# Four head pairs' chains in lockstep instead of two, one chunk a step, and the two directions' outputs stored apart

## The chip, the cores and the metric

The kernel runs on one core of a Trainium2 chip. Its time is the device time of the whole program in microseconds (us): the median of three runs, with the lowest and highest beside it. One further execution was recorded by the hardware profiler. Engines carry the profile's names: PE is the matrix engine (PEld its weight loads), DVE, ACT and POOL the vector, scalar and general engines, SP the queue that issues most loads.

## What is computed

One layer of a backbone over 1024 latent tokens with a prefix of 256 context tokens, width 1024, all in float32. Two branches read the same normalised input; the change touches the first, a bidirectional RWKV-7 scan with 16 heads of 64:

```
def step(S, inp):                                   # one token, state S of 64 x 64 per head
    sa = einsum('bhvk,bhk->bhv', S, kk_t)
    S  = S * w_t - sa b_t + v_t k_t
    o  = einsum('bhvk,bhk->bhv', S, r_t)            # latents only
...
for d in (0, 1):                                    # forward, backward
    S, o = rwkv7_scan(..., S0[d], reverse=(d == 1))
o = head_norm(outs[0] + outs[1], ln_w, ln_b, 16 heads, eps)
o = o + bons[0] + bons[1]
ya = (o * silu(g)) @ w_o
```

The latent scans start from the final state of the context scan of the same direction. The second branch is a retention with four heads, in both directions, with its own norm, gate and projection. Both are merged by two gates, projected, added to the input and normalised.

## The kernel before

**Stages, in order.** Projections of the input and the preparation of the RWKV operands (to about 830 us of the span); the RWKV chains over the context (830 to 1164) together with the projection of retention's values (`gv`); the RWKV chains over the latents (1164 to 1794) together with the gate projections (`gm`); the output stage with retention and the RWKV output projection (1794 to about 2211); the merge and the last projection (to 2497).

**Chains.** The scan runs in chunks of 64 tokens: four chunks of context and sixteen of latents for each head pair and direction. The 16 heads are 8 pairs of two heads, which share the 128 partitions; a pair and a direction make one chain, so there are 16 chains. `chain_step` takes several chains one chunk further. It multiplies the old state by the keys (`X`), ACT negates the result (`xs`), `U` multiplies by the inverse of the chunk's triangular matrix (`T`), ACT copies that (`uv`), `S` and `O` make the new state and the outputs from it, and DVE adds the decayed old state `sp`, which POOL made. These depend on each other one after the other.

**Filling the waits.** Between X, U and S/O stands a gap each: `gap` puts a share of the gate projections' matmuls there, so that PE has work while ACT and DVE copy. The share is the work left over the gaps left. `rwkv_lat` takes two pairs in both directions at a time, four chains, two chunks to a group: 4 x 8 groups of two steps, 64 steps in all. With each step it puts work for the next group: `chunk_mats` (the products `A` of keys with keys and queries, from tiles `ka` and `bk`, evacuated by DVE into `ka` and `aa`, and the scaling of `bk` on POOL), `chunk_turn` (four transposes `bt` of that `bk`, evacuated by ACT), and in `inv_gap` pieces of the inverses that are needed some steps later. `inv_gap` counts gaps, 24 to an inverse: keys (`B`, from `kt` and `bi` tiles) at five of them, the vector work spread over 24 (17 in the first), and two joins (`I`). `inverse` does the same in the context stage; it waits two turns between the vector work and the join.

**Outputs.** `put` copies a finished group's outputs from PSUM into a tile `oT` of two pairs and all 1024 tokens. Whichever direction comes second in a place is added there by DVE. After eight groups `oT` is stored to `oD`, which so holds the sum of both directions.

**The output stage.** `out_a` takes the 1024 tokens in two batches of 512. In each, `rwkv_norm` runs for the eight head pairs: load the tile `ar` from `oD`, split it into two parts (`hi` on ACT, `lo` on POOL), sum over the heads on PE (`mu`, two matmuls), subtract, square, split again, sum (`va`), and scale; then two loads named `bg` (the bonus `bonD` and the gate `gD`), which POOL adds and multiplies. Eight results (`act`) feed the matmuls `ya`. Retention (`st`, `sc`, `ro`, `ktp`, `ot` on PE) stands in the same stage, and the order of the two on each engine is made by a scheduler from the order of recording, priorities and what waits for what; inside the chains the order is that of the code. `bg` tiles have the tag `"ma"` with two buffers, `ar` has two, `hi` and `lo` three.

Of the kernel before, what the change touches and what calls it, by code (L numbers as in the profile page):

```python
# [15 lines left out]
P = 128  # L16
# [33 lines left out]
MF = 2.0  # L50
# [3 lines left out]
VEC = 2.8  # L54
# [74 lines left out]
class Kern:  # L129
# [11 lines left out]
    def run(self, upto=9):  # L141
        nc, tc, ins = self.nc, self.tc, self.ins
        with ExitStack() as ctx:
# [27 lines left out]
            self.oD = dr("oD", [NPAIR, P, LAT])  # L171
# [407 lines left out]
    def phase1b(self):  # L579
        nc, tc = self.nc, self.tc  # L580
        pool = lambda name, **k: tc.tile_pool(name=name, bufs=1, reuse_waits="tile", **k)
        with ExitStack() as c:
# [22 lines left out]
            with pool("wg") as self.wp:  # L605
                self.begin(gates, 3 * 16 * NPAIR // 2, 0.0)
                self.rwkv_lat(*first)
                self.end()

    def begin(self, jobs, gaps, hold):  # L610

        self.left = sum(10 * KT * 3 * 0.107 if size == 2 else 2 * KT * 3 * 0.2135 for size, _ in jobs)
        self.debt, self.gaps, self.hold = 0.0, gaps, hold
        self.work, self.stores = self.filler(jobs), []
        next(self.work)

    def end(self):
        for _ in self.work:
            pass
        self.flush()  # L620
# [73 lines left out]
    def gate_out(self, acc, dst, silu, sp, eng=None):  # L694
# [8 lines left out]
        else:  # L703
            self.stores.append((dst, st))

    def flush(self):

        for dst, st in self.stores:
            self.nc.scalar.dma_start(dst, st)
        self.stores = []  # L710
# [86 lines left out]
    def subs(self, n):  # L797
# [3 lines left out]
        pp, half = divmod(n - 2, 2)  # L801
        return [(p, d, NCU + 8 * half + 4 * q) for q in range(2) for p in (2 * pp, 2 * pp + 1) for d in range(2)]

    def inverse(self, n):
# [146 lines left out]
    def inv_gap(self, t):  # L951
# [4 lines left out]
        per, g = divmod(t, 24)  # L956
        last = 1 + NPAIR
        n = 4 + per
        if g == 1 and n <= last:
# [8 lines left out]
        if t == 0 or g == 17:  # L968
            n = 3 + per + (g == 17)
            self.vec = self.inv_vec(self.jobs[n]) if n <= last else iter(())  # L970
            self.vec_us, self.vec_gaps, self.owed = 12 * TV + sum(map(self.sub_us, range(31))), 24 if t else 17, 0.0
# [6 lines left out]
        if g == 16:  # L978
# [3 lines left out]
    def chunk_loads(self, p, u0, d=None, extra=False):  # L982
# [4 lines left out]
        odd = p % 2 if d is None else d  # L987
        ka = (self.wp if extra else rw).tile([P, 3, 4, C], F32, tag=f"ka{odd}", name=self.nm("ka"), bufs=2 - extra)
# [6 lines left out]
        two = lambda t: t.rearrange("q (d u) c -> q d u c", d=2)  # L995
        nc.sync.dma_start(two(bk), self.bkD[p].rearrange("d q u c -> q d u c")[:, :, u0:u0 + 2, :])
        o = C * (u0 - NCU)
        kr = lambda rows, a: self.krD[p, :, rows, a, o:o + 2 * C].rearrange("d q j -> q d j")
        pair = lambda t: t.rearrange("q (d u) c -> q d (u c)", d=2)
        for h, ch, va in self.HEADS:  # L1000
            nc.sync.dma_start(pair(ka[ch, 2 * h]), kr(ch, 0))
        nc.sync.dma_start(pair(ka[:, 1]), kr(slice(0, P), 1))
        scale = self.pc[:, p, :, u0:u0 + 2].rearrange("q d (u o) -> q d u o", o=1)
        return bk, ka, scale, False

    def chunk_mats(self, loads):
# [5 lines left out]
        if ctx:  # L1012
# [6 lines left out]
            nc.gpsimd.tensor_tensor(bk, bk, scale.broadcast_to([P, 4, 2 * C]), op=ALU.mult)  # L1019
        else:  # L1020
# [11 lines left out]
            b4 = bk.rearrange("q (d u) c -> q d u c", d=2)  # L1032
            nc.gpsimd.tensor_tensor(b4, b4, scale.broadcast_to([P, 2, 2, 2 * C]), op=ALU.mult)
# [13 lines left out]
    def chain_step(self, chains, sv, uv, pcs, extra, new=None, out=None):  # L1047
# [4 lines left out]
        nc, rw = self.nc, self.rw  # L1052
        px = self.pC.tile([P, 4, C], F32, tag="C", name=self.nm("X"))
# [3 lines left out]
        xs = rw.tile([P, 4, C], F32, tag="xs", name=self.nm("xs"), bufs=1)  # L1057
        with self.tc.high_priority(offset=URGENT):
            self.lead("a", nc.scalar.mul(xs, px, -1.0))
        if new is not None:  # L1060
            sp = rw.tile([P, 4, C], F32, tag="sp", name=self.nm("sp"), bufs=1)
# [534 lines left out]
```

## Time and profile before

| | |
|---|---|
| median of 3 runs | 2504.42 us (2503.66 to 2504.76) |
| the profiled execution | 2498.37 us |
| its span | 2496.6 us |
| mean granted PE clock | 0.987 |
| busy PE, PEld | 2386.0, 1926.1 us |
| busy DVE, ACT, POOL | 1649.2, 1162.1, 562.3 us |

The profile is one execution. Busy times of an engine are shares of the span; a PE instruction's duration includes time in which it overlaps the next one, so two starts tell more than a duration. In rows of instruction groups stand the line of the kernel, the engine, the operation with output and inputs, the shapes, the count, the busy time, the mean in ns, and the idle time just before with what ended it. Line 556 is the helper that records all matmuls of the chains and gates, so those are told apart by their tiles. Lines after the edited ones shift by a few in the changed kernel (1316 becomes 1311).

### The profile page before, as it was taken

Reading aid. Unit: us, or ns where it says so; the run is one execution under the profiler, and the core shown is the slowest. Engines: PE = TensorE matmul, PEld = TensorE weight load, DVE = VectorE, ACT = ScalarE, POOL = GpSimd, SP = SyncE. Lnnn points to the kernel's source line nnn. Section 1 sums busy time; section 2 is a strip of 40 time slices with the busy share of each in tenths; the row PEclk is TensorE's granted clock in tenths of the full one; section 3 lists DMA queues with packets and bytes.
Section 4 is the critical chain, followed back from the end, with each engine's and each line's share of the span. In section 5 each row is a group of like instructions: output and inputs, shape, how many; then the busy total and the mean of one; then the engine's idle time right before and its main releaser. Section 6 shows DMA issues by size and latency. Waiting matters only on the chain.

```text
span 2496.6 us, 53437 instructions
## 1 busy us (share of the span) xinstructions
PE 2386.0 (96%) x21200; PEld 1926.1 (77%) x21200; DVE 1649.2 (66%) x2882; ACT 1162.1 (47%) x2547; POOL 562.3 (23%) x688
## 2 busy tenths in 40 slices
PE   7999999999999899997999999999898998999998
PEld 4888888777888899986777777777666765678786
DVE  5497897797796254434887787884378657754644
ACT  6434334334334334444655666554356435543422
POOL 2211021211021001211222322222276335400000
PEclk9999999999999899998999999999999999999999
DMA  6143344343344625354546556554465755585552
GB/s 250 50 149 118 140 152 135 133 141 121 135 156 152 199 88 146 106 139 124 157 145 175 163 170 192 149 160 135 123 187 165 224 160 156 180 285 170 182 174 85
DMA packets 335660, 385.07 MB, mean 154 GB/s; under 512 B 86954, under 2 KB 240306, under 8 KB 331314
## 3 DMA queue, kind: packets, MB, share of 16 engines
q1 hardware_dynamic: 304370, 298.80, 39.0%
q0 software_dynamic: 10944, 55.58, 6.7%
q10 hardware_dynamic: 20096, 27.27, 3.1%
q8 instruction: 167, 2.74, 0.4%
q14 instruction: 83, 0.68, 0.1%
HBM read 264.63 MB, written 116.92 MB: 153 GB/s over the span
## 4 chain that ended last, share of the span: by engine, by line
PE 53%; DMA 5%; DVE 5%; ACT 3%; issue 2%; SPq 2%; POOL 2%; ACTq 0%; DVEq 0%; POOLq 0%
PE gm L556 10%; PE gv L556 7%; PE ro L1475 3%; PE A L556 2%; PE yr L1276 2%; PE yr L1274 2%; PE yr L1275 2%; DMA bi<-bkD 2%; PE S L556 2%; PE X L556 2%; PE bt L1043 2%; PE gm L330 2%; PE gm L332 1%; PE gm L331 1%; PE U L556 1%
## 5 line engine op out<-in xcount | busy, mean ns | idle before, releaser
L330 PE MATMUL gm<-uh,wh 128*128 128x512 f32 x896 | 354.2, 396 | 16.2 <-ACT xp L402 13.7
L331 PE MATMUL gm<-ul,wh 128*128 128x512 f32 x896 | 353.7, 395 | 0.7 <-DVE ul L299 0.7
L332 PE MATMUL gm<-uh,wl 128*128 128x512 f32 x896 | 353.2, 394 | 0.0
L330 PEld LDWEIGHTS gm<-uh,wh 128*128 128x128 f32 x896 | 169.6, 190 | 51.5 <-ACT xp L402 15.0
L1063 POOL TENSOR_TENSOR sp<-sv,pc 64x256 f32<-64x256 f32 x152 | 104.9, 690 | 424.9 <-DVE sv L1087 202.3
L331 PEld LDWEIGHTS gm<-ul,wh 128*128 128x128 f32 x896 | 169.8, 189 | 38.4 <-DVE xnt L298 1.7
L332 PEld LDWEIGHTS gm<-uh,wl 128*128 128x128 f32 x896 | 169.7, 189 | 34.9
L556 PE MATMUL gm<-uh,wlo 128*128 128x512 f32 x416 | 171.0, 411 | 0.7 <-DVE wlo L658 0.7
L556 PE MATMUL gm<-ul,whi 128*128 128x512 f32 x416 | 171.3, 412 | 0.0
L556 PE MATMUL gm<-uh,whi 128*128 128x512 f32 x416 | 170.8, 411 | 0.0
L658 DVE TENSOR_TENSOR wlo<-wraw,whi 128x256 fp32r<-128x256 f32 x168 | 81.0, 496 | 122.5 <-ACT whi L657 121.3
L556 PE MATMUL gv<-whi,uh 128*128 128x256 f32 x512 | 148.7, 290 | 0.3 <-issue 0.3
L211 DVE TENSOR_TENSOR lo<-raw,hi 128x512 fp32r<-128x512 f32 x128 | 92.3, 726 | 85.2 <-ACT hi L210 85.0
L556 PE MATMUL gv<-whi,ul 128*128 128x256 f32 x512 | 147.7, 289 | 0.0
L556 PE MATMUL gv<-wlo,uh 128*128 128x256 f32 x512 | 147.6, 288 | 0.0
L210 ACT CAST hi<-raw 128x512 fp32r<-128x512 f32 x128 | 78.6, 620 | 140.1 <-PE yr L1275 74.1
L902 DVE TENSOR_TENSOR TL<-TL,tmp 128x31 f32<-128x31 f32 (+15 forms) x310 | 135.3, 436 | 8.5
L1077 ACT COPY uv<-U 64x256 f32<-64x256 f32 x160 | 58.6, 366 | 156.3 <-PE U L556 82.7
L900 DVE TENSOR_TENSOR tmp<-E,TL 128x31 f32<-128x31 f32 (+15 forms) x310 | 124.0, 400 | 8.9
L1087 DVE TENSOR_TENSOR sv<-S,sp 64x256 f32<-64x256 f32 x144 | 60.7, 422 | 103.1 <-PE S L556 58.6
L1475 PE MATMUL ro<-s,rs 128*128 128x512 f32 x256 | 123.7, 596 | 4.8 <-DVE s L1429 4.3
L210 ACT CAST wh<-wr 128x1024 fp32r<-128x1024 f32 x56 | 58.8, 1050 | 130.7 <-PE gm L331 127.2
(298 smaller groups left out, 6228.1 us busy)
## 6 DMA issues: line engine op xcount, KB each, us to landing
wr<-in_w_in SPq DMA_DIRECT2D x56, 512.0 KB, 3.5
wraw<-in_w_in SPq DMA_DIRECT2D x84, 256.0 KB, 3.6
bkD<-bk POOLq DMA_DIRECT2D x16, 1280.0 KB, 5.6
bk<-bkD SPq DMA_DIRECT2D x80, 256.0 KB, 3.6
krD<-kr POOLq DMA_DIRECT2D x16, 1024.0 KB, 4.4
raw<-in_wr SPq DMA_DIRECT2D x64, 256.0 KB, 3.1
vtD<-vt POOLq DMA_DIRECT2D x64, 160.0 KB, 3.9
bi<-bkD SPq DMA_DIRECT2D x160, 64.0 KB, 2.6
```

What stands on the lines that cost most here:

```text
L210: nc.scalar.copy(hi, src)
L211: (eng or nc.vector).tensor_tensor(lo, src, hi.bitcast(F32), op=ALU.subtract)
L330: nc.tensor.matmul(acc[:, :n], hi[:, k, :], self.hi(k, t0, n), start=(k == 0), stop=False)
L331: nc.tensor.matmul(acc[:, :n], hi[:, k, :], self.lo(k, t0, n), start=False, stop=False)
L332: nc.tensor.matmul(acc[:, :n], lo[:, k, :], self.hi(k, t0, n), start=False, stop=(k == KT - 1))
L556: return self.pin(self.nc.tensor.matmul(*a, **k))
L658: self.late(nc.vector.tensor_tensor(lo[:, j % size, k:k + 2], r, h.bitcast(F32), op=ALU.subtract), "v")
L900: self.late(nc.vector.tensor_tensor(t3, et[:, j + 1:, j:j + 1].broadcast_to([P, n, m]), tl[:, j:j + 1, 0:m].broadcast_to([P, n, m]), op=AL ...
L902: self.late(nc.vector.tensor_tensor(tl[:, j + 1:, 0:m], tl[:, j + 1:, 0:m], t3, op=ALU.subtract), "v")
L1063: nc.gpsimd.tensor_tensor(sp[ch], sv[ch, h], pcs[ch].broadcast_to([64, 4, C]), op=ALU.mult)
L1087: self.lead("v", nc.vector.tensor_tensor(new[h], ps[ch], sp[ch], op=ALU.add))
L1475: nc.tensor.matmul(po, qx[d][:, k, cols], st[:, k, :], start=(d == 1 and k == 0), stop=False)
```

## The change

**Latents.** `rwkv_lat` takes four pairs in both directions, eight chains, one chunk to a step: 32 steps in place of 64. The order within a step is X, then the first half of the next step's `chunk_mats` and both transposes of the tiles made a step ago, a gap; U and O, the second half of `chunk_mats` and the loads for two steps ahead, a gap; S and O, the outputs, a gap. There are 96 gaps in place of 192, and `inv_gap` counts 12 to an inverse. The transposes of a tile stand a step later than its products now. One `ka`/`bk` tile holds two pairs in both directions at one chunk, not one pair at two chunks, so the loads' contiguous pieces in DRAM halve. The tiles `sv`, `uv`, `xs`, `sp` and the PSUM tiles hold eight chains.

**A.** Each product of 128 x 128 is issued as two with 64 output partitions each, which lie in different parts of the tile of `pA`.

**Outputs.** `oD` has a plane for each direction. `put` copies both directions with ACT into a tile `og` of two steps (the backward one with its tokens reversed); `send` stores it on POOL's queue a step later, with four stores to a tile, 64 in all. `rwkv_norm` loads both planes, the second into a tile `back`, and POOL adds them; `back` has the tag `"ma"`.

**Constants and timing.** `MF` (gate work in the prologue of the latents) 2.0 to 5.0, `VEC` 2.8 to 4.2, the first fill of the first inverse in the contexts 2.5 times as long, five idle turns instead of two before an inverse's join, and stores of gate results two gaps later.

```diff
-MF = 2.0
+MF = 5.0
-VEC = 2.8
+VEC = 4.2
-            self.oD = dr("oD", [NPAIR, P, LAT])
+            self.oD = dr("oD", [2, NPAIR, P, LAT])
-                self.begin(gates, 3 * 16 * NPAIR // 2, 0.0)
+                self.begin(gates, 3 * 16 * NPAIR // 4, 0.0)
...
     def inverse(self, n):
-        yield
-        yield
+        for _ in range(5):
+            yield
         yield from self.inv_join(job)
     def rwkv_ctx(self):
-        for _ in self.inverse(0):
-            self.fill(HEAD)
+        for i, _ in enumerate(self.inverse(0)):
+            self.fill(HEAD if i else 2.5 * HEAD)
...
     def inv_gap(self, t):
-        per, g = divmod(t, 24)
+        per, g = divmod(t, 12)
-        if g in (1, 4, 7, 10, 13) and n <= last:
+        if g in (0, 1, 4, 7, 10) and n <= last:
             next(self.keys)
-        if g in (19, 22) and 3 + per <= last:
-            if g == 19:
-                self.join = self.inv_join(self.jobs[3 + per])
+        if g == 11 and 3 + per <= last:
+            self.join = self.inv_join(self.jobs[3 + per])
+        if (g == 11 and 3 + per <= last) or (g == 0 and 0 < per and 2 + per <= last):
             next(self.join)
...
-            self.vec_us, self.vec_gaps, self.owed = 12 * TV + sum(map(self.sub_us, range(31))), 24 if t else 17, 0.0
+            self.vec_us, self.vec_gaps, self.owed = 12 * TV + sum(map(self.sub_us, range(31))), 11, 0.0
...
     def chunk_loads(self, p, u0, d=None):
-        nc.sync.dma_start(two(bk), self.bkD[p].rearrange("d q u c -> q d u c")[:, :, u0:u0 + 2, :])
+        nc.sync.dma_start(bk, self.bkD[p:p + 2, :, :, u0, :].rearrange("a d q c -> q (a d) c"))
...
     def chunk_mats(self, loads):
             for i in range(4):
-                for h, ch, va in self.HEADS:
-                    self.mm(pas[h][:, i], bk[ch, i, :], ka[ch, h:h + 2, i, :], start=True, stop=True)
+                for c in (slice(0, C), slice(C, 2 * C)):
+                    for h, ch, va in self.HEADS:
+                        self.mm(pas[h][c, i], bk[ch, i, c], ka[ch, h:h + 2, i, :], start=True, stop=True)
...
     def lat_loads(self, n, a):
-        pp, g = divmod(n, 8)
-        return self.chunk_loads(2 * pp + a, NCU + 2 * g, None, not a and n % 3 == 2)
+        r, u = divmod(n, 16)
+        return self.chunk_loads(4 * r + 2 * a, NCU + u)
...
     def rwkv_lat(self, ld, vals):
+        for n in range(last + 1):
+            r, s = divmod(n, 16)
...
+            def turns():
+                self.send(outs)
+                if n < last:
+                    nxt.append(self.chunk_mats(ld.pop(0)))
+                for m in mats:
+                    self.chunk_turn(m)
+                self.inv_gap(3 * n)
+
+            def products():
+                if n < last:
+                    nxt.append(self.chunk_mats(ld.pop(0)))
+                    if n + 1 < last:
+                        ld.extend(self.lat_loads(n + 2, a) for a in range(2))
+                self.inv_gap(3 * n + 1)
+
+            def outputs():
+                self.put(po, og, s)
+                if s % 2:
+                    outs.append((r, s, og))
+                self.inv_gap(3 * n + 2)
...
+            self.chain_step(chains, sv, uv, pcs, (turns, products, outputs), dst, po)
...
-    def put(self, po, oT, g):
-            if g < 4:
-                nc.scalar.copy(o, src)
-            else:
-                nc.vector.tensor_tensor(o, src, o, op=ALU.add)
+    def put(self, po, og, s):
+        src = po.rearrange("p (a d) c -> p a d c", d=2)
+        self.nc.scalar.copy(og[:, 0, :, s % 2], src[:, :, 0])
+        self.nc.scalar.copy(og[:, 1, :, 1 - s % 2], src[:, :, 1][:, :, ::-1])
+
+    def send(self, outs):
+        for r, s, og in outs:
+            for d, t0 in ((0, C * (s - 1)), (1, LAT - C * (s + 1))):
+                for h, ch, va in self.HEADS:
+                    self.nc.gpsimd.dma_start(self.oD[d, 4 * r:4 * r + 4, ch, t0:t0 + 2 * C].rearrange("p q t -> q p t"),
+                                             og[va, d].rearrange("q p u c -> q p (u c)"))
+        outs.clear()
...
     def rwkv_norm(self, p, t0, ps):
-        self.load(x, self.oD[p][:, t0:t0 + 512])
+        self.load(x, self.oD[0, p][:, t0:t0 + 512])
+        back = self.wp.tile([P, 512], F32, tag="ma", name=self.nm("back"), bufs=2)
+        self.load(back, self.oD[1, p][:, t0:t0 + 512])
+        nc.gpsimd.tensor_tensor(x, x, back, op=ALU.add)
```

**The order on the engines.** First PE in the middle of the latents: one step from X to the first B, with the shape and the number of equal instructions at the end of a row. Before:

```order
L556 MATMUL X_17313<-sv_16994,ka_16818 64x64 x4
L556 MATMUL X_17313<-sv_16994,ka_16975 64x64 x4
L556 MATMUL A_17328<-ka_17164,bk_17163 128x128
L556 MATMUL A_17329<-ka_17164,bk_17163 128x128
...
L556 MATMUL gm_17247<-uh_100,whi_16834 128x512
...
L556 MATMUL gm_17247<-uh_101,wlo_16835 128x512
L556 MATMUL U_17355<-xs_17322,T_1721_14396 64x64 x2
L556 MATMUL O_17306<-ka_16818,sv_16994 64x64 x2
...
L556 MATMUL B_17374<-kt_17215,bi_17216 64x64 x2
```

Now:

```order
L556 MATMUL X_12299<-sv_11995,ka_11843 64x64 x8
L556 MATMUL X_12299<-sv_11995,ka_11849 64x64 x8
L556 MATMUL A_12326<-ka_12146,bk_12145 64x128
L556 MATMUL A_12327<-ka_12146,bk_12145 64x128
...
L1041 MATMUL bt_12350<-ident,bk_11842 128x128 x4
L1041 MATMUL bt_12357<-ident,bk_11848 128x128 x4
L556 MATMUL gm_12211<-ul_112,whi_11765 128x512
...
L556 MATMUL U_12393<-xs_12316,T_1072_9864 64x64 x2
L556 MATMUL O_12297<-ka_11843,sv_11995 64x64 x2
...
L556 MATMUL A_12429<-ka_12152,bk_12151 64x128
...
L556 MATMUL B_12465<-kt_12175,bi_12176 64x64 x2
```

X, U and O have twice the instructions, A has sixteen with 64 output partitions where eight with 128 stood, transposes follow A, and twelve gate matmuls stand between there and U where six stood.

Second, PE at the normalisations `mu` and `va` of the second batch. Before (the fifth of the eight pairs; `st` and `ktp` are retention's):

```order
L217 MATMUL mu_25129<-hi_25130,ones 128x512
L1414 MATMUL st_23778<-vt_23755,kx_23763 128x512
L1415 MATMUL st_23778<-vt_23755,kx_23763 128x512
...
L1395 MATMUL ktp_23800<-ident,rs_23788 128x128 x4
L218 MATMUL mu_25129<-lo_25131,ones 128x512
L1414 MATMUL st_23809<-vt_23792,kx_23805 128x512
```

Now, from the second of the eight pairs to the third, and from the last to the first matmuls that read the results:

```order
L218 MATMUL mu_25251<-lo_25253,ones 128x512
L1411 MATMUL ro_24466<-vt_23896,sx_24463 128x512
L1495 MATMUL ot_24497<-ident,on_24426 128x128 x4
L217 MATMUL va_25261<-hi_25262,ones 128x512
L218 MATMUL va_25261<-lo_25263,ones 128x512
L1495 MATMUL ot_24510<-ident,on_24474 128x128 x4
L217 MATMUL mu_25286<-hi_25287,ones 128x512
L218 MATMUL mu_25286<-lo_25288,ones 128x512
...
L217 MATMUL va_25471<-hi_25472,ones 128x512
L1266 MATMUL ya_25491<-act_25243,hi_25493 128x512
L1267 MATMUL ya_25491<-act_25243,hi_25493 128x512
```

Between the third pair's `mu` and the last pair's `va` stand only `mu` and `va` rows; before, retention's rows stood between the `mu` and `va` of each pair.

Third, POOL at the same place. Before (L1506 and L1408 are retention's):

```order
L211 TENSOR_TENSOR lo_25195<-ar_25191,hi_25194 128x512
L1316 TENSOR_TENSOR ar_25159<-ar_25159,bg_25182 128x512
L1316 TENSOR_TENSOR ar_25159<-ar_25159,bg_25185 128x512
L1506 TENSOR_TENSOR on_23902<-on_23902,gr_24022 128x512
L1408 TENSOR_TENSOR rs_24098<-rs_24096,qd_23861 128x512
L1408 TENSOR_TENSOR rs_24100<-rs_24096,qd_23861 128x512
L1506 TENSOR_TENSOR on_23950<-on_23950,gr_24070 128x512
L211 TENSOR_TENSOR lo_25227<-ar_25223,hi_25226 128x512
L1316 TENSOR_TENSOR ar_25191<-ar_25191,bg_25214 128x512
```

Now:

```order
L1295 TENSOR_TENSOR ar_25281<-ar_25281,back_25283 128x512
L211 TENSOR_TENSOR lo_25288<-ar_25281,hi_25287 128x512
L1311 TENSOR_TENSOR ar_25281<-ar_25281,bg_25307 128x512
L1311 TENSOR_TENSOR ar_25281<-ar_25281,bg_25310 128x512
L1295 TENSOR_TENSOR ar_25316<-ar_25316,back_25318 128x512
L211 TENSOR_TENSOR lo_25323<-ar_25316,hi_25322 128x512
```

The next pair's `lo` stood ahead of the `bg` additions of the pair before it; now both `bg` rows of a pair come first, and then the next pair's `back`.

More of the change, by code (lines that the diff above doesn't have):

```diff
@@ L613, in begin @@
         self.debt, self.gaps, self.hold = 0.0, gaps, hold
-        self.work, self.stores = self.filler(jobs), []
+        self.work, self.stores = self.filler(jobs), [[], [], []]
         next(self.work)
@@ L619, in end @@
             pass
-        self.flush()
+        for _ in self.stores:
+            self.flush()
     def gap(self):
@@ L703, in gate_out @@
         else:
-            self.stores.append((dst, st))
+            self.stores[-1].append((dst, st))
     def flush(self):
-        for dst, st in self.stores:
-            self.nc.scalar.dma_start(dst, st)
-        self.stores = []
+        for dst, st in self.stores[0]:
+            self.late(self.nc.scalar.dma_start(dst, st), "a")
+        self.stores = self.stores[1:] + [[]]
     def gate_proj(self, ct, dst, silu, wp, gps, sp):
@@ L800, in subs @@
             return [(p, d, 0) for p in range(4 * n, 4 * n + 4) for d in range(2)]
-        pp, half = divmod(n - 2, 2)
-        return [(p, d, NCU + 8 * half + 4 * q) for q in range(2) for p in (2 * pp, 2 * pp + 1) for d in range(2)]
+        r, q = divmod(n - 2, 4)
+        return [(p, d, NCU + 4 * q) for p in range(4 * r, 4 * r + 4) for d in range(2)]
     def inverse(self, n):
@@ L1056, in chain_step @@
                 self.mm(px[ch, ci, :], ka[:, 2 * h, :], sv[:, h, ci, :], start=True, stop=True)
[L1057 removed]
+        xs = tile("xs")
         with self.tc.high_priority(offset=URGENT):
@@ L1070, in chain_step @@
             if out is not None:
-                po, first, last = out
                 for h, ch, va in self.HEADS:
-                    self.mm(po(va, ci), sv[ch, h, ci, :], rho[ch], start=(first and ci == 0), stop=False, skip_group_check=True)
+                    self.mm(out[va, ci], sv[ch, h, ci, :], rho[ch], start=(ci == 0), stop=False, skip_group_check=True)
         with self.tc.high_priority(offset=URGENT):
@@ L1080, in chain_step @@
         if new is not None:
-            ps = self.pC.tile([P, 4, C], F32, tag="C", name=self.nm("S"))
+            ps = psum("S")
             for ci, (ka, rho, aa, bt, t2) in enumerate(chains):
@@ L1090, in chain_step @@
                 for h, ch, va in self.HEADS:
-                    self.mm(po(va, ci), uv[:, h, ci, :], aa[:, h, :], start=False, stop=(last and ci == 3), skip_group_check=True)
+                    self.mm(out[va, ci], uv[:, h, ci, :], aa[:, h, :], start=False, stop=(ci == m - 1), skip_group_check=True)
         extra[2]()
@@ L1132, in chain_ctx @@
             else:
-                end = rw.tile([P, 4, C], F32, tag="xs", name=self.nm("send"), bufs=1)
+                end = rw.tile([P, 8, C], F32, tag="xs", name=self.nm("send"), bufs=1)[:, :4]
                 dst = [end[ch] for h, ch, va in self.HEADS]
@@ L1174, in rwkv_lat @@
         ld = [self.lat_loads(1, a) for a in range(2)]
-        for m in mats:
-            self.chunk_turn(m)
-            next(keys)
+        for _ in keys:
             self.fill(MF)
-        for n, (pp, g) in enumerate(groups):
-            if g == 0:
-                oT = self.wp.tile([P, 2, LAT], F32, tag="oT", name=self.nm("oT"), bufs=1)
-            more = n + 1 < len(groups)
-            svt, uvt = vals
-            po = self.pO.tile([P, 4, 2, C], F32, tag="O", name=self.nm("O"))
+        last, og, outs = 2 * 16 - 1, None, []
@@ new lines, in rwkv_lat @@
+        for n in range(last + 1):
+            r, s = divmod(n, 16)
+            t2 = self.t2[2 + 4 * r + s // 4]
+            chains = [(ka[:, :, i], ka[:, 1, i], aa[:, :, i], bt[:, i], t2[a][:, 4 * i + s % 4, :])
+                      for a, (ka, aa, bt, bk) in enumerate(mats) for i in range(4)]
+            sv, uv = vals
+            if n < last:
+                vals = self.lat_values(n + 1)
+            dst = [vals[0][ch, h] for h, ch, va in self.HEADS] if s < 15 else None
+            pcs = self.pc[:, 4 * r:4 * r + 4, :, NCU + s:NCU + s + 1].rearrange("q p d o -> q (p d) o")
+            po = self.pO.tile([P, 8, C], F32, tag="O", name=self.nm("O"))
@@ new lines, in turns @@
+                self.inv_gap(3 * n)
+            def products():
+                if n < last:
+                    nxt.append(self.chunk_mats(ld.pop(0)))
[7 more added lines that the diff above has]
+                self.inv_gap(3 * n + 2)
+            if s % 2 == 0:
+                og = self.wp.tile([P, 2, 4, 2, C], F32, tag="og", name=self.nm("og"), bufs=2)
```

101 lines of the change are left out of this document (30 added, 71 removed).

## The prediction

> **What bounds the kernel now.** I read the page's busy times first, then the windows of 50 us over the whole span, then the timeline of one latent step, then who waited for whom, and last the instruction groups of the output stage.
>
> ```profile
> span 2496.6 us, 53437 instructions
> PE 2386.0 (96%) x21200; PEld 1926.1 (77%) x21200; DVE 1649.2 (66%) x2882; ACT 1162.1 (47%) x2547; POOL 562.3 (23%) x688
> ```
>
> Two windows carry it: one in the latents, one in the second batch of normalisations. The columns are the window, its length, busy PE, PEld, DVE, ACT, POOL, then the granted clock, the DMA share and GB/s.
>
> ```profile
> 1500.00:1550.00 50.00, 48.32 (x744) 37.95 (x744) 39.27 (x93) 30.68 (x93) 13.65 (x16) 1.00 0.64 183
> 2100.00:2150.00 50.00, 46.88 (x199) 31.22 (x198) 42.68 (x72) 27.33 (x64) 28.35 (x23) 1.00 0.41 127
> ```
>
> TensorE is busy for 48.3 of 50 us in the first and 46.9 in the second, at full clock. So PE's own row of instructions is the bound in both places, and the change is worth what it takes off that row, less what it leaves PE to wait for. Matmul durations overlap and say little; I cost PE by the distance from one start to the next.
>
> **The latents: hand-overs.** One step and a bit, PE alone (start, duration, instruction):
>
> ```profile
> 1504.93 0.69 PE L556 MATMUL S<-uv,bt 128*64 128x64 f32 x16
> 1505.45 0.64 PE L556 MATMUL O<-aa,uv 128*64 128x64 f32 x16
> 1506.02 0.66 PE L1043 MATMUL bt<-ident,bk 128*128 128x128 f32 x4
> 1506.43 0.47 PE L556 MATMUL gm<-uh,wlo 128*128 128x512 f32 x1
> ...
> 1507.99 0.69 PE L556 MATMUL X<-sv,ka 128*64 128x64 f32 x16
> 1508.61 1.16 PE L556 MATMUL A<-ka,bk 64*128 64x128 f32 x16
> 1509.70 0.50 PE L556 MATMUL gm<-uh,wlo 128*128 128x512 f32 x1
> 1510.03 0.40 PE L556 MATMUL gm<-uh,whi 128*128 128x512 f32 x1
> ...
> 1510.96 0.39 PE L556 MATMUL gm<-ul,whi 128*128 128x512 f32 x1
> 1511.28 0.27 PE L556 MATMUL U<-xs,T 64*64 64x64 f32 x2
> ...
> 1511.80 0.41 PE L556 MATMUL B<-kt,bi 64*64 64x64 f32 x16
> ```
>
> Between 1510.03 and 1510.96 lie four starts, 0.23 us per gate matmul. The run of six from 1509.70 takes 1.58 us until U starts, which is 6 x 0.23 + 0.20; the run from 1506.43 takes 1.56. So a run of gate matmuls pays about 0.20 us of hand-over, however long it is. S and X are the same 16 instructions: S takes 0.52 us until O, which has the same tile shape (128*64), and X takes 0.62 until A, which has another. A change of shape among the small products costs 0.10 us.
>
> A step has three gate runs and four shape changes among small products: before X to A, A to gm, U/O to gm, O to bt; now X to A, A to bt, A to gm, O to gm. Steps fall from 64 to 32. That saves 96 x 0.20 = 19 us and 4 x 32 x 0.10 = 13 us, **32 us** in all. Everything else on PE is the same products in longer runs. The gate matmuls stay 48 per weight tile; the larger MF moves 56 of them ahead of the first step and changes no sum.
>
> **The quartered A products** have no row before. U and O are 32 instructions of 64*64 with 64 moved columns and take 0.52 us (1511.28 to 1511.80), 0.065 per four: four tiles work at once. With 128 columns that is 0.13 per four, 8 x 0.13 = 1.04 us for the 32 new instructions, plus 0.10 at a shape change where one follows. A takes 1.09 with its change now. I take **0**. From the other side, if only two worked at once, the run would take about 0.9 us more, 62 times: +57 us. U/O have the new shape exactly, so I stay at the first.
>
> **Waits that lose their cause.** PE's own waits in the latents (1196 to 1796 us) and in the contexts and the start of the latents (820 to 1196 us): waiting line and tile, what it waited for, us in total, times, longest.
>
> ```profile
> PE S L556 <- ACT uv L1077: 5.1, 5, 1.6
> PE B L556 <- DMA bi<-bkD: 4.7, 9, 1.7
> ```
>
> ```profile
> PE B L556 <- DMA bi<-bkD: 9.0, 10, 2.8
> PE I L556 <- DVE TN L910: 7.7, 2, 7.2
> ```
>
> S now follows twelve gate matmuls (2.8 us) after U instead of six or seven, while the copies to uv double in columns only; B's next loads are issued three gaps of some 5.4 us ahead instead of 2.9. I take 8 of these 9.8 us. In the second pair the first fill grows from 2.4 to 6 us, MF from 2 to 5, and three more turns lie between the last vector work and the join: I take 13 of 16.7. Bounds: nothing, and all 26.5. Together **-21 us**.
>
> **Stores, loads and evacuations.** The outputs go out by 64 stores on POOL, four every two steps. They stand ahead of the scaling of bk there, which is needed a step later.
>
> ```profile
> L1222 POOL DMA_DIRECT2D oD<-oT x4 | 2.2, 548 | 14.0 <-DVE oT L1234 14.0
> ```
>
> At 0.55 us each that is 35 us of POOL over some 520, on an engine busy for 13.7 of 50: I take 0, since a whole step of 16 us covers them; without that cover each group of four (2.2 us) would delay bt, 16 x 2.2 = 35 us. Each step's two ACT copies into og take the place of one copy or one DVE addition per two steps; ACT is at 30.7 of 50 and DVE loses work, so 0 as well. SP issues as many loads as before, but their runs in DRAM halve (512 to 256 bytes, bk 1024 to 512).
>
> ```profile
> ka<-krD SPq DMA_DIRECT2D x118, 64.0 KB, 3.3
> bi<-bkD SPq DMA_DIRECT2D x100, 64.0 KB, 2.7
> ```
>
> These are KB each and median us to landing: bi already moves 64 KB in runs of 256 bytes and lands in 2.7 us, ka moves 64 KB in runs of 512 and needs 3.3. By these rows shorter runs cost nothing, and a load has a step to arrive. The Trainium skill (DMA: Bandwidth & Descriptors, Specifications) speaks against this part: it wants at least 512 bytes per transfer for line rate, and says that below it the engine does a read-modify-write. By that rule the sum would be worse (third rival); by the two rows it is unchanged.
>
> **The output stage** pays. `back` takes its buffer from the two of the tag "ma", which the bon and g loads of the same head pair use up. So the load of `back` for pair p+1 waits until POOL has added bon of pair p, and the whole chain of a normalisation follows it. Its steps, from the groups of 1820 to 2170 us (line, engine, out<-in, forms, count | busy us, mean ns | idle before), with the load's median landing first:
>
> ```profile
> ar<-oD SPq DMA_DIRECT2D x16, 256.0 KB, 3.3
> L1316 POOL TENSOR_TENSOR ar<-ar,bg 128x512 f32<-128x512 f32 x32 | 42.4, 1323 | 51.1 <-DVE ar L1312 43.0 <-DMA bg<-gD 5.0 <-DMA gr<-grD 2.2
> L210 ACT CAST hi<-ar 128x512 fp32r<-128x512 f32 x16 | 9.9, 619 | 10.0 <-DMA ar<-oD 9.6
> L211 POOL TENSOR_TENSOR lo<-ar,hi 128x512 fp32r<-128x512 f32 x16 | 21.4, 1340 | 25.4 <-ACT hi L210 25.3
> L218 PE MATMUL mu<-lo,ones 128*128 128x512 f32 x16 | 7.6, 478 | 3.4 <-POOL lo L211 3.4
> L1304 DVE SCALAR_TENSOR_TENSOR ar<-mu,ar 128x512 f32<-128x512 f32 x16 | 10.9, 683 | 2.9 <-PE mu L218 2.9
> L1306 ACT ACTIVATE sq<-ar 128x512 f32<-128x512 f32 x16 | 10.1, 633 | 9.5 <-DVE ar L1304 7.9 <-DVE ar L1311 0.8 <-DVE bmv L1491 0.8
> L210 ACT CAST hi<-sq 128x512 fp32r<-128x512 f32 x16 | 9.9, 618 | 0.3
> L211 DVE TENSOR_TENSOR lo<-sq,hi 128x512 fp32r<-128x512 f32 x16 | 15.6, 973 | 6.6 <-ACT hi L210 6.6
> L218 PE MATMUL va<-lo,ones 128*128 128x512 f32 x16 | 7.1, 445 | 0.1
> L1309 ACT ACTIVATE sq<-va,eps 128x512 f32<-128x512 f32 x16 | 11.0, 685 | 2.4 <-PE va L218 2.3
> L1310 ACT ACTIVATE sq<-sq 128x512 f32<-128x512 f32 x16 | 10.1, 631 | 0.3
> L1311 DVE TENSOR_TENSOR ar<-ar,sq 128x512 f32<-128x512 f32 x16 | 11.8, 737 | 1.6 <-ACT sq L1310 1.5
> L1312 DVE TENSOR_SCALAR ar<-ar,ph 128x512 f32<-128x512 f32 x16 | 11.1, 693 | 0.0
> ```
>
> Load 3.3, the new addition as L1316 1.32, then 0.62, 1.34, 0.48, 0.68, 0.63, 0.62, 0.97, 0.45, 0.69, 0.63, 0.74 and 0.69, and bon's addition 1.32: **14.5 us from one head pair to the next**, one at a time. Before, two overlapped.
>
> In the first batch of eight PE's order still has retention between the mu and va rows, so the chain is covered there; but the batch lasts longer and uses up retention that used to cover the second. In the new order one last `ot` of retention follows the second pair's va in the second batch; after it PE holds only mu and va of six more pairs, and the next matmuls of ya read all eight results. From there PE sees 6 x 14.5 = 87 us, then the last multiplication by g and its split (1.32 + 0.62 + 0.97 = 2.9), and has 24 mu and va rows and 12 of ya to do, 36 x 0.23 = 8.3 us. That leaves **82 us of idle PE** where the window at 2100 had 3 in 50. All of PE's other work there stays, so it adds in full. The eight new loads and POOL additions of each batch are inside the chain. From below, were the load always early: 11.2 per pair, 62 us. From above, with a fifth more for queueing behind retention's last instructions (an estimate): 17.4 per pair, 99 us.
>
> **Sum**, against the profiled execution of 2498.37 us (its span is 2496.6): -32 - 21 + 82 = +29, 2527 us. The median of the timed runs is 2504.42, 6 above that execution, so I forecast **2533 us** for the median. The case's own range: -32 - 26.5 + 62 = +3 to -32 + 99 = +67.
>
> **Rivals.**
> *Not slower: the chain is short.* The point is the pitch of the second batch. With 53 us gained ahead of it, break-even is 6P + 2.9 - 8.3 = 53, P = 9.7 us. At 9 us a pair the run ends 4 us below today, at 2500. For it: POOL and DVE were shared with retention when these means were taken, and are free in the tail. Against it: the compute rows alone, without the load, sum to 11.2.
> *DVE becomes the bound of the latents.* The vector work of an inverse goes into 11 of every 12 gaps. DVE's 39.3 of 50 is 13.8 us per two old steps of 17.6 (eight A evacuations among them), and the new step is to take about 16; an 87% full queue in order could hold up A's four PSUM buffers. At 1.5 us a step in 24 steps, +36: 2569.
> *Loads late.* If a run of 256 bytes takes a DMA engine as long as one of 512, the share of 0.64 in the window at 1500 nears 1 in a shorter step, and the step falls back to its 17.6 us: the 32 us are lost, 2565. Against it stand ka and bi above. This is the case that the Trainium skill's 512 bytes would make.
> *The quartering does not pay as four tiles* (the change does not do what it says): +57, 2590.
>
> **Chances.** Forecast 0.70, short chain 0.07, DVE 0.12, loads 0.08, quartering 0.03. Range **2506 to 2568**: below it lies most of the short chain, above it the quartering and half of DVE's case. A difference under 0.2% (5 us) cannot be told from none here. Faster by more: 0.06 (most of the short chain); within: 0.06 (its rest and the lowest end of the forecast's range); slower: 0.88.
>
> **What would show it.** Right: the second batch's windows show PE nearly idle for 75 to 95 us, with mu and va 14 us apart and POOL waiting for DMA `back`; a latent step near 16 us; gate runs of twelve at 2.96 us; A runs near 1.1 us; the 7.2 us wait before I gone. Wrong: retention or ya matmuls between the second batch's mu rows, a pitch under 10 us, a step of 17 us or more, or S and A waiting for DVE.

## The result and the profile after

The changed kernel takes 2591.23 us (median of 4 runs, 2588.21 to 2596.74) against 2504.04 us before: a ratio of 1.0354, with a 95% interval of 1.0332 to 1.0377. It is slower, by 87 us where 29 were forecast. The profiled execution took 2590.98 us, 92.6 more than that of before.

The page of the changed kernel, span, busy times and the granted clock in 40 slices (tenths of full speed):

```profile
span 2589.2 us, 55461 instructions
PE 2384.3 (92%) x22224; PEld 1941.9 (75%) x22224; DVE 1633.1 (63%) x2790; ACT 1155.7 (45%) x2483; POOL 603.5 (23%) x704
PEclk9999999999999999999999999999999997599999
```

PE is busy for the same time as before (2386.0) in a span that is 93 us longer: the change added waiting, not busy time. Two slices show a lower clock. In the windows of the changed kernel (window, length, busy PE, PEld, DVE, ACT, POOL, clock, DMA share, GB/s), two from the latents and two from the second batch of normalisations:

```profile
1250.00:1300.00 50.00, 41.05 (x928) 34.19 (x927) 33.47 (x77) 28.61 (x69) 14.26 (x17) 0.93 0.56 140
1500.00:1550.00 50.00, 47.13 (x937) 38.40 (x930) 39.73 (x87) 26.52 (x70) 17.16 (x21) 0.97 0.64 166
...
2150.00:2200.00 50.00, 21.09 (x60) 10.50 (x58) 18.01 (x31) 17.34 (x41) 20.51 (x16) 0.66 0.57 189
2200.00:2250.00 50.00, 9.32 (x12) 3.44 (x12) 11.76 (x18) 13.20 (x21) 17.68 (x14) 0.50 0.21 69
```

The last two are the foretold gap: PE busy for 9 of 50 us, at half clock. The first two were not foretold: the latents lose time too, and the clock falls there as well, where it was 1.00 from 1200 us on to the end of the latents before.

**Where the 92.6 us come from.** The trace gives three points in each kernel: the start of the last `O` of the chains, that of the last `ya`, and the end of the span. All runs told of below are listed with them (us).

| kernel | to the last `O` | from there to the last `ya` | from there to the end | time, median |
|---|---|---|---|---|
| before | 1791.7 | 429.9 | 274.9 | 2504.0 |
| changed | 1792.6 | 516.9 | 279.7 | 2591.2 |
| 1: `back` in another buffer | 1791.1 | 454.3 | 284.0 | 2535.0 |
| 2: order on DVE | 1761.1 | 515.0 | 280.3 | 2562.3 |
| 3: both | 1767.1 | 456.4 | 283.0 | 2510.0 |
| 4: second plane left out | 1791.0 | 434.2 | 277.0 | 2504.1 |
| 5: order on DVE, adding stores | 1763.3 | 434.6 | 275.5 | 2475.2 |
| 6: adding stores | 1797.2 | 433.0 | 276.1 | 2505.9 |
| 7: old timing of the contexts | 1788.5 | 517.2 | 280.7 | 2588.4 |
| 8: as 5, A not split | 1777.5 | 436.6 | 275.5 | 2491.6 |
| 9: as 5, old timing of the contexts | 1769.0 | 433.1 | 275.8 | 2479.8 |

The output stage lost 87 us (82 forecast). The contexts and latents, forecast 53 us shorter, end where they ended.

For the stretch from 825 us to the last `O`, every distance between two PE starts can be put into one of three: time in which no matmul runs, what a matmul takes longer in the pieces recorded at half clock than one of its kind outside, and the rest, the work itself at full clock.

| 825 us to the last `O` | work at full clock | no matmul running | lost to the half clock |
|---|---|---|---|
| before | 919 | 37 | 11 |
| changed | 882 | 60 | 26 |
| 2: order on DVE | 883 | 39 | 14 |

The work fell by 37 us, about as the counting of hand-overs said (32). The waits, forecast to fall by 21, grew by 23, and the clock took 15 more. Nearly all of that arose in the latents: from 1196 us on, the time without a matmul grew from 13.0 to 37.5 us, and the loss to the half clock from nothing to 13.5.

**What PE waits for in the changed latents** (1196 to 1796 us; waiting line and tile, what it waited for, us in total, times, longest; "issue" stands where the profile shows nothing that PE waited for):

```profile
PE I L556 <- DVE aa L1030: 19.1, 6, 6.8
PE A L556 <- PE O L556: 6.7, 13, 1.0
PE I L556 <- issue: 5.0, 3, 2.0
```

The waits of S for uv and of B for its loads, which were costed, are gone from this list. New ones stand in their place. One of the six waits of I, on DVE and on PE (start, duration, instruction):

```profile
1424.20 2.28 DVE L895 STREAM_TRANSPOSE E<-D 128x256 f32<-128x256 f32 x4
1426.51 0.20 DVE L901 TENSOR_TENSOR tmp<-E,TL 128x31 f32<-128x31 f32 x1
...
1432.84 0.38 DVE L903 TENSOR_TENSOR TL<-TL,tmp 128x207 f32<-128x207 f32 x1
1433.24 0.43 DVE L1029 TENSOR_TENSOR ka<-A,mask 64x256 f32<-64x256 f32 x1
1433.68 0.42 DVE L1030 TENSOR_TENSOR aa<-A,mask 128x256 f32<-128x256 f32 x1
```

```profile
1427.49 1.10 PE L556 MATMUL A<-ka,bk 64*64 64x128 f32 x32
1428.53 1.09 PE L1041 MATMUL bt<-ident,bk 128*128 128x128 f32 x8
1434.26 2.05 PE L556 MATMUL I<-T 32*32 32x32 f32 x128 [4.64 <-DVE aa L1030]
```

A is done by 1428.6. DVE evacuates it (ka, aa) from 1433.24 on, since the next inverse stands ahead of it in DVE's queue: the transposes to E and nine pairs of tmp and TL. The two tiles of A and the two of bt hold all four buffers of the tag "A", so I, the fifth and sixth tile, waits for A's. Before, one `chunk_mats` (two tiles) came in a step's first gap and one `chunk_turn` (one tile) in its third, so A's tiles had two gaps longer to be emptied.

**The output stage.** In the trace of before, the first batch of normalisations takes 113 us from its first `mu` to its last `va`, the second 124; in the changed kernel they take 182 and 143. The longer first batch runs beside retention, whose work is then missing beside the second.

From one pair's `back` to the next pair's `mu` (all engines):

```profile
2206.60 1.26 POOL L1295 TENSOR_TENSOR ar<-ar,back 128x512 f32<-128x512 f32 x1 [1.39 <-DMA back<-oD]
2207.90 0.62 ACT L210 CAST hi<-ar 128x512 fp32r<-128x512 f32 x1 [2.04 <-POOL ar L1295]
2208.57 0.79 PE L217 MATMUL mu<-hi,ones 128*128 128x512 f32 x1 [8.73 <-ACT hi L210]
...
2216.47 0.55 DVE L1307 TENSOR_SCALAR ar<-ar,ph 128x512 f32<-128x512 f32 x1
2217.10 2.60 POOL L1311 TENSOR_TENSOR ar<-ar,bg 128x512 f32<-128x512 f32 x2 [7.24 <-DVE ar L1307]
...
2221.03 1.26 POOL L1295 TENSOR_TENSOR ar<-ar,back 128x512 f32<-128x512 f32 x1 [1.33 <-DMA back<-oD]
...
2223.00 0.79 PE L217 MATMUL mu<-hi,ones 128*128 128x512 f32 x1 [8.67 <-ACT hi L210]
```

The pitch from `mu` to `mu` is 14.43 us, against 14.5 forecast. Of each, PE waits 8.7 us for the next `mu`, 0.6 for its second matmul and 2.1 for `va`. The next pair's load of `back` goes out at 2218.39, when POOL has added the bonus of this pair, and the addition that needs it starts at 2221.03. The matmuls that remain take 0.79 us each, at half clock.

### The profile page after: what moved, and what is told of

The parts are those of the page before. It is cut to its first block, busy times and chain, and to the rows that moved or that the text cites. A ratio compares the mean times of both kernels' runs of the same rounds, so it can differ in the third digit from the quotient of the medians.

```text
span 2589.2 us, 55461 instructions
## 1 busy us (share of the span) xinstructions
PE 2384.3 (92%) x22224; PEld 1941.9 (75%) x22224; DVE 1633.1 (63%) x2790; ACT 1155.7 (45%) x2483; POOL 603.5 (23%) x704
## 5 line engine op out<-in xcount | busy, mean ns | idle before, releaser
L659 DVE TENSOR_TENSOR wlo<-wraw,whi 128x256 fp32r<-128x256 f32 x168 | 91.6, 568 | 189.1 <-ACT whi L658 183.1
L1063 POOL TENSOR_TENSOR sp<-sv,pc 64x512 f32<-64x512 f32 (+1 forms) x92 | 90.2, 981 | 302.4 <-DVE sv L1086 239.8
L1031 POOL TENSOR_TENSOR bk<-bk,pc 128x512 f32<-128x512 f32 x80 | 86.7, 1084 | 269.9 <-PE A L556 182.5
L901 DVE TENSOR_TENSOR tmp<-E,TL 128x31 f32<-128x31 f32 (+15 forms) x310 | 116.4, 375 | 9.2
L1424 DVE SCALAR_TENSOR_TENSOR s<-s,ph,st 128x512 f32<-128x512 f32 x128 | 90.3, 739 | 35.2 <-PE st L1411 31.1
```

Source lines behind the costliest of these rows:

```text
L659: self.late(nc.vector.tensor_tensor(lo[:, j % size, k:k + 2], r, h.bitcast(F32), op=ALU.subtract), "v")
L901: self.late(nc.vector.tensor_tensor(t3, et[:, j + 1:, j:j + 1].broadcast_to([P, n, m]), tl[:, j:j + 1, 0:m].broadcast_to([P, n, m]), op=AL ...
L1063: nc.gpsimd.tensor_tensor(sp[ch], sv[ch, h], pcs[ch].broadcast_to([64, m, C]), op=ALU.mult)
L1424: nc.vector.scalar_tensor_tensor(new[:, k], old[:, k], self.cd[:, d, h:h + 1], a, op0=ALU.mult, op1=ALU.add)
```

## The experiments

**1. `back` in a buffer of its own.** One edit in `rwkv_norm`:

```diff
-        back = self.wp.tile([P, 512], F32, tag="ma", name=self.nm("back"), bufs=2)
+        back = self.wp.tile([P, 512], F32, tag="raw", name=self.nm("back"), bufs=WR)
```

> Only the buffer of `back` changes: it takes the tag of the raw weights (three buffers, idle during the normalisations) in place of "ma". Theory A (the load of the next pair's `back` waits for POOL's addition of the bonus of the pair before, and that makes the normalisations serial): two pairs overlap again, mu rows of the second batch no longer stand 14.5 us apart, the 95.6 us of half clock at 2166 shrink to under 40, and the time falls by 40 to 75 us, to 2516 to 2551. Rival B (the chain itself is too long, whatever the buffers, because POOL has one more addition to do for each pair): under 20 us are won, over 2571. The latents stay as they are, with some 37 us of idle PE in both cases.

2535.01 us, a ratio of 1.0124 (1.0098 to 1.0151): 56 us less than the changed kernel, within theory A's range. The time to the last `O` did not move (1791.1). Four rows of PE in the second batch, in order of start:

```profile
2177.64 0.79 PE L217 MATMUL mu<-hi,ones 128*128 128x512 f32 x1 [3.47 <-ACT hi L210]
...
2183.71 0.80 PE L217 MATMUL va<-hi,ones 128*128 128x512 f32 x1 [2.26 <-ACT hi L210]
...
2192.31 0.79 PE L217 MATMUL mu<-hi,ones 128*128 128x512 f32 x1 [7.08 <-ACT hi L210]
...
2197.06 0.79 PE L217 MATMUL va<-hi,ones 128*128 128x512 f32 x1 [2.15 <-ACT hi L210]
```

Retention still stands beside the normalisations until 2174 us. The first batch takes 127 us instead of 182, the second 111 instead of 143, and some pairs overlap again: the first `mu` of one starts before the last `va` of the pair before it (1833.0 and 1833.7 us). In the output stage PE now idles for 45 us, where it was 97 in the changed kernel and 26 before, and the half clock of the tail lasts 34.1 us in place of 95.6. So the shared buffer made the normalisations serial, and serial they outlast retention. Two things stay. The last pairs do not overlap: their first `mu` rows start at 2163.55, 2177.64 and 2192.31, still 14.1 and 14.7 us apart, which theory A did not foretell. At 2175.50 POOL's addition waits 4.4 us there for the load of `ar`, which has two buffers too; that this is the reason was not tried. And 24 us of the 87 stay: this edit alone does not restore the output stage.

**2. The evacuation of A ahead of the inverse on DVE.** The scheduler keeps work that is recorded as late behind the last instruction named as lead; aa becomes that one:

```diff
-                nc.vector.tensor_tensor(aa[:, h], pa[:, :, 1 - h], m, op=ALU.mult)
+                self.lead("v", nc.vector.tensor_tensor(aa[:, h], pa[:, :, 1 - h], m, op=ALU.mult))
```

> Only the order on DVE changes: the evacuations of A (ka, aa) are made the point behind which inverse work that is recorded later has to stand. Theory C (in the changed latents PE waits at I and at the second A for the four PSUM buffers of tag "A", which DVE frees late because pieces of an inverse stand ahead of ka and aa): the waits of I behind bt (19.1 us) and of A behind O (8.3 us) go, with them most of the 13.5 us that the halved clock costs; 25 to 40 us less, 2551 to 2566. Rival D (DVE simply has too much to do there): the wait moves to the join's first part, I for TN, and under 10 us are won. Rival E (the loads in pieces of 256 bytes are late): nothing changes. The output stage keeps its 97 us of idle PE in all cases.

2562.31 us, 1.0232 (1.0212 to 1.0253): 29 us less. PE's waits in its latents (1196 to 1765 us), the largest three:

```profile
PE I L556 <- issue: 6.0, 5, 2.1
PE B L556 <- ACT bt L1043: 5.5, 9, 1.3
PE X L556 <- issue: 4.7, 3, 3.7
```

The 19.1 us of I for aa and the waits of A are gone, and I for TN, the wait that rival D put in their place, has 0.7. Here ka follows A at once, and I follows the transposes:

```profile
1419.40 0.43 DVE L1029 TENSOR_TENSOR ka<-A,mask 64x256 f32<-64x256 f32 x1 [2.41 <-PE A L556]
1419.84 0.43 DVE L1030 TENSOR_TENSOR aa<-A,mask 128x256 f32<-128x256 f32 x1
```

DVE does the same instructions in another order, so it was the order and not the amount that PE paid for. By the second table 21 us of what is gained up to the last `O` (31) are waits and 12 are the clock, and the work is 1 us more. Rival E, late loads, falls with it: nothing about the loads was touched.

**3. Both edits.**

> Both edits together. If the output stage and the latents lose separately, the gains add: 2451 to 2526, on the likeliest values (58 and 32 us) 2501, about the kernel before. If one lengthens the other, the sum is missed by over 15 us.

2510.02 us, 1.0015 (0.9999 to 1.0031): 81 us less than the changed kernel, where the single gains add to 85. The two losses are separate. The kernel is as fast as before, no faster.

**4. Without the second plane.** The load of `back` and its addition are taken out; the outputs of the backward scan are missing from the sum.

```diff
-        back = self.wp.tile([P, 512], F32, tag="ma", name=self.nm("back"), bufs=2)
-        self.load(back, self.oD[1, p][:, t0:t0 + 512])
-        nc.gpsimd.tensor_tensor(x, x, back, op=ALU.add)
```

> The second direction's plane is neither loaded nor added in the output stage (the outputs of the backward scan are left out of the sum); the latents still store both planes. Theory A: the output stage takes what it took before, some 430 us from the last O of the chains to the last ya, 87 us less than with the addition, 2504 in all, since the latents gained nothing. If the output stage is long for another reason (the larger tiles of the latents, stores of og still in flight), it stays above 470 us and the time above 2545.

2504.09 us (one run). The output stage takes 434.2 us. So 83 of the 87 us that the output stage lost belong to these three lines, and some 4 at most to the 64 stores or the larger tiles. The load of the second plane and its addition were not told apart here. The lockstep of four pairs, with the output stage of before, gives no time.

**5. The directions added by the stores, with the order edit.** One plane of `oD` again. The stores of a half's steps 8 to 15 add to what the first eight steps wrote, and `rwkv_norm` loads one tile as before:

```diff
+                    more = {"accum_op": ALU.add} if s > 8 else {}
-                    self.nc.gpsimd.dma_start(self.oD[d, 4 * r:4 * r + 4, ch, t0:t0 + 2 * C].rearrange("p q t -> q p t"),
-                                             og[va, d].rearrange("q p u c -> q p (u c)"))
+                    self.nc.gpsimd.dma_start(self.oD[4 * r:4 * r + 4, ch, t0:t0 + 2 * C].rearrange("p q t -> q p t"),
+                                             og[va, d].rearrange("q p u c -> q p (u c)"), **more)
```

> The order edit on DVE of the earlier run, and the two directions added by the stores themselves: one plane in DRAM, the stores of steps 0 to 7 of a half write, those of steps 8 to 15 add to what lies there (an accumulating store on POOL's queue); the output stage loads one tile and has no `back`. If the two causes named so far (serial normalisations, A's buffers) are all that the change lost, the output stage takes the 430 us that it took without the second plane and the latents end at 1761: 2504 - 29 = 2475 us, within 6, faster than the kernel before by 1.2%. If adding stores are slow or hold up POOL's queue, bk is scaled late, bt waits on PE, and 32 stores of some extra us each show as waits at bt: over 2490.

2475.18 us, 0.9886 (0.9865 to 0.9906): faster than both kernels, by 1.1% than the one before, and at the forecast value. Its window of the second batch, and its stores:

```profile
2100.00:2150.00 50.00, 50.00 (x206) 32.78 (x205) 41.19 (x70) 28.07 (x71) 27.96 (x21) 1.00 0.57 176
```

```profile
oD<-og POOLq DMA_DIRECT2D x64, 128.0 KB, 4.4
```

PE has no gap there. A store lands in 4.4 us at the median, where the plain ones of the changed kernel took 3.5; nothing on PE waits for it.

**6. Adding stores alone.**

> Adding stores alone, without the order edit: the lockstep with the output stage of before. As the latents of the changed kernel ended where those of before did, 2504 us, within 6 of the kernel before. If the tail hid some loss elsewhere, or adding stores cost something, it is above 2512.

2505.91 us, 1.0008 (0.9993 to 1.0022), no different from before. With experiment 5 beside it, the order edit is worth 31 us here, as it was worth 29 on the changed kernel. It was not run on the kernel before, where PE idles for only 13 us between 1196 us and the last `O`.

**7. The context stage's timing of before**, on the changed kernel:

```diff
-VEC = 4.2
+VEC = 2.8
-        for _ in range(5):
-            yield
+        yield
+        yield
-            self.fill(HEAD if i else 2.5 * HEAD)
+            self.fill(HEAD)
```

> The changed kernel with the context stage's timing of before (VEC 2.8, two idle turns in place of five, the first fill of the first inverse not lengthened; MF stays 5). Reading F: the constants remove the wait of 7.2 us before I and two others at B, and what they bring (3.2 before I, 2.4 before U, 1.9 and 1.9 before B, and 12.1 instead of 10.3 us at the halved clock) is about as large, so the time stays within 5 us of 2591. Reading G, as predicted: without them 8 to 13 us are lost, 2599 to 2604. If they cost time, it is under 2584.

2588.43 us, 1.0332 (1.0309 to 1.0356). It is reading F: these constants are worth nothing that can be told from nothing, and not the 13 us of the prediction. MF and the later stores of gate results were not tried. The changed kernel's waits from 820 to 1196 us show where the gain went:

```profile
PE B L556 <- DMA bi<-bkD: 9.3, 10, 2.1
PE I L556 <- DVE TN L911: 4.3, 2, 3.2
PE U L556 <- ACT xs L1059: 2.4, 1, 2.4
```

I waits for TN for 4.3 us where it was 7.7, but B waits as before (9.0), and U has a wait that was not there. In experiment 7 I waits for TN for 7.4 us again and B for 7.1, and the time is no longer for it.

**8. A not split**, on the kernel of experiment 5:

```diff
-                for c in (slice(0, C), slice(C, 2 * C)):
-                    for h, ch, va in self.HEADS:
-                        self.mm(pas[h][c, i], bk[ch, i, c], ka[ch, h:h + 2, i, :], start=True, stop=True)
+                for h, ch, va in self.HEADS:
+                    self.mm(pas[h][:, i], bk[ch, i, :], ka[ch, h:h + 2, i, :], start=True, stop=True)
```

> The fastest kernel so far (order edit and adding stores) with A as before, 128 output partitions in 16 instructions instead of 64 in 32. Reading H (four tiles of 64*64 work at once, and A then has the shape of U, O and B around it): without the split a run of A takes 1.09 us instead of 1.04, 62 times, and one or two changes of shape of 0.10 us come back at each second A: 6 to 13 us longer, 2481 to 2488. Reading I, the rival of the prediction (only two tiles at once): without the split it is faster, under 2470.

2491.60 us, 0.9950 (0.9932 to 0.9968): 16 us longer than with the split, so reading I falls, and H is short by 4 to 11 us. A run of A takes 1.09 us from its start to that of the next instruction:

```profile
1512.16 1.16 PE L556 MATMUL A<-ka,bk 64*128 64x128 f32 x16
1513.25 1.09 PE L1040 MATMUL bt<-ident,bk 128*128 128x128 f32 x8
```

With the split it is 1.04 (1427.49 to 1428.53 above). Over 61 runs that is 3 us, and U/O into A costs 0.11 us more at each of 31 places, another 3. The rest, some 10 us, is not work: the half clock took 11 us of the latents instead of 6, and I waits longer, by the largest entry of PE's waits there

```profile
PE I L556 <- issue: 12.6, 6, 4.4
```

against 5.8 us for the same entry in experiment 5. The scheduler orders DVE anew for this kernel, so these waits cannot be put down to the split itself.

**9. The context stage's timing of before, on the kernel of experiment 5.**

> The fastest kernel so far with the context stage's timing of before (as in the earlier run). If the context constants are worth nothing, 2475 within 5 us; the latents and the output stage keep their lengths.

2479.79 us, 0.9904 (0.9889 to 0.9919). Its interval overlaps that of experiment 5; the 5 us between the two are not clear of the noise.

## Why the prediction was right in its sign and wrong in its size

**The hand-overs were right.** Forecast 32 us, measured 37 less work at full clock, of which the split of A has about 6. A run of twelve gate matmuls takes 2.95 us to the start of what follows (median of 88 runs; forecast 2.96). The first and the last of one run, and what follows it:

```profile
1511.99 0.50 PE L556 MATMUL gm<-uh,wlo 128*128 128x512 f32 x1
...
1514.64 0.39 PE L556 MATMUL gm<-ul,whi 128*128 128x512 f32 x1
1514.95 0.27 PE L556 MATMUL U<-xs,T 64*64 64x64 f32 x2
```

**The split of A was right:** nothing was forecast, 1.04 us a run was measured where it was 1.09, and by experiment 8 it saves some 6 us of work. The rival on it forecast 2590 us, almost the time that was measured; that is chance, since no run of A became longer.

**Stores and loads were right.** No wait of PE names ka, bk or a store. The loads do cost the DMA engines more, which showed nowhere else; before and then changed, the same stretch:

```profile
1300.00:1350.00 50.00, 48.34 (x914) 37.84 (x906) 39.88 (x101) 30.77 (x78) 12.61 (x17) 1.00 0.60 171
```

```profile
1300.00:1350.00 50.00, 46.78 (x954) 38.92 (x953) 41.55 (x91) 31.10 (x83) 14.53 (x16) 1.00 0.79 204
```

The DMA share rises from 0.60 to 0.79 here, and from 0.54 to 0.64 between 1200 and 1790 us, where the rate goes from 157 to 166 GB/s. So a byte took about a tenth more of the DMA engines' time. By the Trainium skill (DMA: Bandwidth & Descriptors, Specifications) pieces under 512 bytes lose line rate. The share may be that; no wait of PE came of it.

**The waits that lose their cause were wrong: this is the step that failed.** It gave -21 us, 13 in the contexts and the start of the latents and 8 in the latents. Measured are 1 us less without a matmul in the first (24 to 23) and 24 more in the second; the waits grew by 23 in all, and the clock took 15. The working looked only at waits that were in the trace of before and asked which of them would go. The waits of S and B in the latents went, as forecast, and the 7.2 us before I became 3.2; in the contexts B waited on (9.3 for 9.0), and new waits took up the rest. It did not ask which waits the new order within a step would make. The rival on DVE had the answer: it named "A's four PSUM buffers" behind a DVE queue in order, at +36 us, and gave it 0.12. Measured are 27.4 us of waits of I and A (19.1, 6.7, 1.6) and 13.5 us of half clock in the latents, 41 in all; with experiment 2 the latents have 18 us less of waits and 9 less of half clock, since other waits came up. The rival's reason was only half right: DVE was not too full (experiment 2 does the same work without the wait). The order would have told it: on PE, A, bt and I stand behind one another with two tiles each and four buffers; on DVE, pieces of an inverse stand ahead of ka and aa. Both rows were there to be read. The prediction had named the sign of this, a step of 17 us or more: from X to X a step takes 18.8 us on average, where near 16 was expected; two steps of before take 19.0.

**The output stage was right.** The pitch was forecast at 14.5 us and is 14.43, the loss at 82 and is 87. The path is the forecast one, load behind bonus; that the pitch fits to a tenth is partly luck, since the load takes 2.6 us of it instead of 3.3 and the rest 11.8 instead of 11.2. What the loss is made of was not foreseen: from the last `O` to the last `ya` idle PE grew by 71 us, not 82, and the half clock took 15 us more. Experiment 4 shows the cause to be the second plane, and experiment 1 the shared buffer to be most of it.

**The sum:** +1 us up to the last `O` (work -37, waits +23, clock +15) where -53 was forecast, +87 for +82, and +5 after the last `ya`. That end was not in the sum: 18 `yr` matmuls that ran among the last `ya` before now follow them. Together +92.6, where +29 was forecast. With the rival on DVE the prediction itself came to +65 (2569 for the median); the 28 us from there are the waits and the clock up to the last `O` (+38 in all, where that rival and the waits that go made +15), 5 in the output stage and 5 behind it, less 5 by which the work fell further. No case had a price for the half clock.

One statement of the part before the prediction needs mending: the tags "hi" and "lo" have five buffers in the output stage, not three. Nothing was worked out from it.

## What to carry to other kernels

When work is merged into longer steps, list what the merged step holds in each buffer ring at once, tile by tile, and read on the evacuating engine's queue what stands ahead of the evacuation; a saved hand-over is easily given back there, as 37 us were here. A sum that is moved into a later stage wants a buffer of its own there: here a new load with the tag of the last operands of a chain made the chains serial, on engines that were far from full on average. The buffer was most of that loss and not all of it. And if the sum can ride on a store that is made anyway, it may cost nothing: the adding stores took the addition off the output stage, and with the order edit the merged kernel came out 1.1% ahead.

## What the runs showed of the hardware

**A wait can cost more than itself.** In the changed kernel's latents one wait of I and what follows it:

```profile
1274.00:1281.10 7.10, 0.34 (x4) 0.12 (x2) 6.54 (x19) 1.51 (x4) 2.78 (x4) 0.82 0.53 157
1281.10:1285.30 4.20, 4.19 (x133) 3.74 (x134) 1.20 (x4) 2.08 (x4) 1.92 (x4) 0.50 0.02 4
```

PE waits 6.8 us, and the clock stands at half from 1278.5 to 1285.3, for its last 4.2 us with PE fully busy again. All pieces at half clock after 800 us but the last of each kernel last 3.4 us or a multiple; from 1196 us to the last `O` the changed kernel has seven, the kernel before none. They followed waits of 6.8, 4.6 and 3.1 us, and also shorter ones (2.2, 2.0, 1.7 and 1.3 us, all at I, whose matmuls are small), while single waits of 1.6 us (before A) and 1.9 us (before I) drew none. In the tail the clock stood at half for 95.6 us, with PE busy for 24.8 of them:

```profile
2166.00:2261.60 95.60, 24.82 (x40) 11.53 (x41) 25.96 (x39) 30.50 (x54) 32.77 (x26) 0.50 0.38 129
```

The Trainium skill (TensorE: Matmul & The Clock Gate, Part 1) says that the clock falls to half after an idle window of about 3.4 us. The length of the pieces agrees; the waits under 2.3 us that drew one do not, as far as this trace shows.

**The adding stores cost no time that can be told from noise.** Experiment 6 differs from experiment 4 only in adding the second direction in the stores, and takes 2505.91 us against 2504.09 (one run), though a store lands in 4.3 us at the median instead of 3.3.
